# The first layer's output projection as seven half-size products

## The chip, the core and the metric

The kernel runs on one core of a Trainium2 chip. TensorE (PE) multiplies, and its weight loads (PEld) run beside; VectorE (DVE), ScalarE (ACT) and GpSimd (POOL) do everything else on 128-partition tiles, and SyncE (SP) issues the transfers. The metric is the device time of one execution in microseconds, the median of several runs.

## What is computed

Two layers of a diffusion backbone over 512 latent tokens and 256 context tokens of width 1024. The first layer (differential attention) ends, for all 768 tokens, in

```python
o = rms_norm(o, subln_g) * (1.0 - lam_init)
return (o * jax.nn.silu(gate)) @ w_out          # 768 x 1024 times 1024 x 1024
...
x = x + gate * rms_norm(y, post_g[i])           # the same for the context, with cgate
```

and the second layer starts with `h = rms_norm(x, pre_g[i]) * (1.0 + scale) + shift` and its projection to queries, keys, values and gates. The change concerns the product with `w_out` of the first layer.

## The kernel before

**Precision.** Every fp32 operand of a matmul is kept as two parts, a high one (a cast on ACT) and a low one (the difference, a subtraction on DVE or POOL). `mm3` (L142 to L145) multiplies high by high, high by low and low by high into one PSUM tile, so each product of a 128x128 block costs three matmuls.

**Weights.** `WStream` hands out weight tiles in the order in which they were added: `wsplit` loads 512 KB into one of two `raw` buffers (L211, on SP's queue), casts the high part on ACT (L213) and makes the low part with `pieces` (L205 to L207), for `w_out` on DVE. Three slots hold the finished pairs; a fourth comes with the pool `bp`, which is opened when the attention of the first layer has been written out.

**The projection.** The gated attention output is held transposed in eight tiles `gT[0..7]` (128 of the 1024 branch columns by 768 tokens), with high and low parts in `ghi` and `glo` (L1027). `OUTC` cuts the 1024 output columns into three blocks: 0 to 256, 256 to 512 and 512 to 1024. For each block and each of six token tiles of 128 (four latent, two context), 8 column groups `kt` of the contraction times three matmuls fill one PSUM tile. The first block is begun early: `out_early` runs seven of the eight `kt` of all six token tiles among the last head's attention, as filler on PE. The rest follows when `gT[7]` is there.

**After each block.** DVE multiplies the PSUM tile by the layer's gate into `u0` (L1219) or `u1` (L1234), ACT takes the sum of squares (`sumsq`, L1204). In the last block `resid_a` and `resid_b` follow each token tile: POOL forms the reciprocal root (L396, L397), DVE adds the scaled tile to the residual row (L1244), which was loaded from x or the context into `x1`, `gate1` and `gacc` at L1171 and L1174, ACT and POOL normalize that row again for the second layer (L1204, L1250). Two token tiles later `h1_tr` transposes it on PE (L1261), scales and shifts it on DVE and ACT (L1266 to L1269) and splits it (L1271, L1272) into `h1hi` and `h1lo`, the operands of the second layer's projections. That next stage runs in the order of the list `KV`: keys and values of token tile t (`k`, `v`), the late transposes (`t`), finishing steps (`c`) and steps of the second layer's gate (`g`).

**What sets the order.** Within the attention a list scheduler (`flow`) with due times writes out the steps; from the projection on the order is written by hand. A tile framework then places each engine's instructions by a time line of its own, so that the order on an engine can differ from that of the text. On the chip each engine runs its own list strictly in that order and waits on semaphores.

## Time and profile before

| | |
|---|---|
| runs, median (3 runs) | 824.65 us (824.65 to 824.75) |
| span of the profiled execution | 822.0 us |
| median less span | 2.65 us |
| PE busy | 792.7 us (96%) |
| DVE busy | 482.3 us (59%) |
| ACT busy | 457.1 us (56%) |
| POOL busy | 440.4 us (54%) |

The span is that of one execution taken by the hardware profiler, and the runs are timed apart from it; what is left lies outside the first and the last instruction. Busy shares are averages over stages with different limits, so a stage has to be looked at by itself: the projection begins at 459.15 us and the next stage's first projection at 538.07. In rows of the time line the first two numbers are the start and the length in us, then come engine, line of the kernel, operation, output and inputs, shapes and count; in brackets stands the idle time before and what ended it. In rows of groups the numbers behind the bar are busy us and mean ns of one, then the idle time before them. A row of a window has, for each engine, its busy us and its number of instructions, then the granted clock, the share of the DMA engines' time and the GB/s.

### The profile page before, as it was taken

The numbers are of one execution on the slowest core, as the hardware profiler recorded it, in microseconds if no ns is written. First come the engines' busy times: TensorE is split into PE (matmuls) and PEld (weight loads), VectorE is DVE, ScalarE is ACT, GpSimd is POOL, SyncE is SP. The second block draws the span as 40 slices with busy tenths as digits, with TensorE's granted clock in tenths as the row PEclk, the third lists the DMA queues.
The fourth block names the chain that finished last, engine by engine and source line by source line (L and its number), as shares of the span: only waits on it lengthen the run. The fifth ranks groups of instructions, "written<-read, shape, count | busy, mean of one in ns | idle before, by whom it ended". The sixth has DMA issues, their size and how long they took to land. (4 is left out here: it accounts for less than half of the span.)

```text
span 822.0 us, 14412 instructions
## 1 busy us (share of the span) xinstructions
PE 792.7 (96%) x5482; PEld 703.0 (86%) x5482; DVE 482.3 (59%) x896; ACT 457.1 (56%) x1001; POOL 440.4 (54%) x538
## 2 busy tenths in 40 slices
PE   7999999999999999999999999999999999999997
PEld 5678897788887898787988898889999899898986
DVE  3425566754768524675458952579546566755534
ACT  6534357664575544765556852674446576666631
POOL 4544766856367744665822311587788656733101
PEclk9999999999999999999999999999999999999999
DMA  9934211122053321323330045033421210301102
GB/s 300 347 131 142 77 39 52 52 77 90 28 154 98 122 101 65 116 78 118 113 104 26 27 151 182 1 110 103 154 79 52 78 52 1 103 26 52 50 28 103
DMA packets 41540, 77.77 MB, mean 95 GB/s; under 512 B 3584, under 2 KB 18688, under 8 KB 41472
## 3 DMA queue, kind: packets, MB, share of 16 engines
q1 hardware_dynamic: 38048, 71.71, 26.4%
q10 hardware_dynamic: 3424, 5.15, 1.8%
q8 instruction: 43, 0.70, 0.3%
q14 instruction: 25, 0.20, 0.1%
HBM read 70.56 MB, written 2.10 MB: 88 GB/s over the span
## 5 line engine op out<-in xcount | busy, mean ns | idle before, releaser
L207 POOL TENSOR_TENSOR wlo<-raw,whi 128x256 fp32r<-128x256 f32 x200 | 152.0, 792 | 72.8 <-ACT whi L213 63.1
L143 PE MATMUL bk<-whi,h 128*128 128x256 f32 (+1 forms) x592 | 176.9, 302 | 1.1 <-ACT p L1459 0.8
L144 PE MATMUL bk<-wlo,h 128*128 128x256 f32 (+1 forms) x592 | 176.2, 299 | 0.2 <-DVE wlo L207 0.2
L145 PE MATMUL bk<-whi,h 128*128 128x256 f32 (+1 forms) x592 | 175.4, 299 | 0.2 <-DVE h L1272 0.2
L143 PE MATMUL bk<-h,whi 128*128 128x512 f32 (+2 forms) x416 | 147.4, 354 | 2.7 <-ACT sq L979 1.5
L144 PE MATMUL bk<-h,whi 128*128 128x512 f32 (+2 forms) x416 | 144.8, 348 | 0.0
L145 PE MATMUL bk<-h,wlo 128*128 128x512 f32 (+2 forms) x416 | 144.8, 348 | 0.0
L143 PEld LDWEIGHTS bk<-whi,h 128*128 128x128 f32 x592 | 112.6, 191 | 8.2 <-issue 2.8
L145 PEld LDWEIGHTS bk<-whi,h 128*128 128x128 f32 x592 | 112.0, 190 | 4.7 <-issue 0.8
L144 PEld LDWEIGHTS bk<-wlo,h 128*128 128x128 f32 x592 | 112.3, 190 | 3.9 <-DVE wlo L207 0.4
L221 POOL TENSOR_SCALAR p<-p,sm 128x768 f32<-128x768 f32 (+1 forms) x80 | 67.1, 842 | 76.5 <-DVE sm L1460 28.7
L143 PEld LDWEIGHTS bk<-h,whi 128*128 128x128 f32 x416 | 78.2, 188 | 15.1 <-issue 4.0
L213 ACT CAST whi<-raw 128x1024 fp32r<-128x1024 f32 x64 | 67.1, 1048 | 36.1 <-PE bk L144 17.7
L145 PEld LDWEIGHTS bk<-h,wlo 128*128 128x128 f32 x416 | 78.3, 188 | 8.8 <-issue 1.6
L144 PEld LDWEIGHTS bk<-h,whi 128*128 128x128 f32 x416 | 78.4, 188 | 7.2 <-issue 0.8
L888 ACT ACTIVATE p<-sc,sm 128x768 f32<-128x768 f32 (+1 forms) x68 | 59.7, 881 | 37.9 <-DVE sm L885 37.9
L885 DVE TENSOR_REDUCE sm<-sc 128x1 f32<-128x768 f32 (+1 forms) x68 | 60.3, 917 | 17.4 <-PE sc L880 17.3
L181 POOL TENSOR_TENSOR sz<-sz,za 128x384 f32<-128x384 f32 (+1 forms) x24 | 28.1, 1172 | 42.8 <-ACT za L180 42.7
L896 DVE SCALAR_TENSOR_TENSOR p<-p,sm,p 128x768 f32<-128x768 f32 (+1 forms) x34 | 40.1, 1179 | 16.5 <-POOL p L221 14.9
L1480 DVE TENSOR_TENSOR al<-bk,ah 128x512 fp32r<-128x512 f32 x48 | 32.6, 687 | 26.1 <-ACT ah L1479 25.9
L950 ACT CAST ah<-bk 128x512 fp32r<-128x512 f32 x56 | 31.7, 590 | 27.9 <-PE bk L945 24.4
L880 PE MATMUL sc<-qk,qk 64*128 64x384 f32 (+1 forms) x396 | 45.8, 354 | 1.1 <-ACT p L888 1.0
(247 smaller groups left out, 1693.0 us busy)
## 6 DMA issues: line engine op xcount, KB each, us to landing
raw<-in_a_w SPq DMA_DIRECT2D x30, 512.0 KB, 3.6
araw<-in_ada_w SPq DMA_DIRECT2D x12, 1024.0 KB, 5.6
raw<-in_b_w SPq DMA_DIRECT2D x20, 512.0 KB, 3.5
ag<-in_ada_w SPq DMA_DIRECT2D x32, 256.0 KB, 6.9
raw<-in_w_out SPq DMA_DIRECT2D x16, 512.0 KB, 3.5
sw<-qr ACTq DMA_DIRECT2D x32, 128.0 KB, 2.5
gw<-in_ada_w SPq DMA_DIRECT2D x8, 512.0 KB, 3.8
xt<-in_x SPq DMA_DIRECT2D x4, 512.0 KB, 5.3
```

Source lines behind the costliest of these rows:

```text
L143: nc.tensor.matmul(o, ahi, bhi, start=start, stop=False)
L144: nc.tensor.matmul(o, ahi, blo, start=False, stop=False)
L145: nc.tensor.matmul(o, alo, bhi, start=False, stop=stop)
L207: eng.tensor_tensor(dst[:, i:i + n], a[:, i:i + n], b[:, i:i + n], op)
L213: nc.scalar.copy(hi, r)
L221: (nc.vector if eng == "v" else nc.gpsimd).tensor_scalar(dst, src, s_, 1.0, ALU.mult, ALU.mult)
L880: prev = nc.tensor.matmul(sc[m][:, j if nk == T else m, :w], a[r, tok], b[r, c], start=i == 0, stop=i == 2)
L885: nc.vector.tensor_reduce(mx, scv, AX.XY if nk == T else AX.X, ALU.max, negate=True)
L888: nc.scalar.activation(pv_, scv, AF.Exp, bias=mx, accum_out=l[:, m:m + 1])
L896: nc.vector.scalar_tensor_tensor(ps_[0], pt, r, ps_[0], ALU.mult, ALU.add)
L950: nc.scalar.copy(ah, tr)
L1480: nc.vector.tensor_tensor(al, tr, f32(ah), ALU.subtract)
```

## The change

The product is done by a scheme of Strassen's kind. Tokens, contraction and output columns are each cut in two halves (384 tokens, 512, 512), and seven products of 384 x 512 x 512 take the place of eight. Their order is `PRODS = (1, 5, 2, 6, 7, 4, 3)`; each has three token tiles, four `kt` and three matmuls of 512 columns (`prod_mm`). P1 and P2 use quarters of both operands as they are.

- Weights: fourteen half-quarters instead of eight pieces. `wprod` loads a quarter into `raw` (P1, P2, P5, P3) or takes it from six rows `xr`, into which `wq_load` put three quarters; P5, P6, P7 and P3 use sums or differences of quarters, P5's on POOL and the others on DVE (`EPR`). All low parts are made on DVE. The residual rows of x and the context are loaded into the same six rows after P6.
- Left operands: P6, P7 and P4 use differences of the halves of `gT`. `t_split` makes each with a subtraction on DVE, a cast on ACT and a subtraction on DVE, twelve times on 128x384. For P5 `gate_mul` subtracts on POOL in pieces, for heads 0 to 3.
- Results: P1's and P5's PSUM tiles are copied out on ACT (`s1`, `s5`), and P6 goes on accumulating in P1's banks; P6's sums are copied to `u2`. Nine additions of 128x512 on DVE join products (`s1`, `s5`, `u2`). The gate multiply of six of the twelve half rows is done on POOL (`part`).
- `out_early` runs P1 and P5, which need `gT[0..3]` alone.
- The tiles `h1hi`, `h1lo` are each cut in two halves, `h1_tr` lags by `HL = 3` token tiles, and the list `KV` is another.

```diff
-KV = (('k', 0), ('k', 1), ('k', 2), ('k', 3), ('t', 4), ('v', 0), ('v', 1), ('t', 5), ('k', 4), ('c', 0), ...
+KV = (('k', 0), ('t', 3), ('v', 0), ('k', 1), ('t', 4), ('v', 1), ('k', 2), ('t', 5), ('v', 2), ('k', 3), ('c',, ...
+EPR = {1: ('', 'v'), 5: ('p', 'v'), 2: ('', 'v'), 6: ('v', 'v'), 7: ('v', 'v'), 4: ('', 'v'), 3: ('v', 'v')}
+ETS = {2: 'v', 3: 'v', 4: 'v'}
+HL = 3
...
+    def wprod(half, prod, pool, slot, key):
+        def load(kq, nq):
+            r = wp.tile([P, 1024], F32, tag="raw", name=nm("raw"), bufs=2)
+            wq_load(r, kq, nq, half)
+            return r
+
+        es, el = EPR[prod]
+        if prod in (1, 2):
+            r = load(prod - 1, 0)
+        elif prod == 5:
+            r, t = load(0, 1), load(1, 1)
+            pieces(VP[es], r, r, t, ALU.add)
+        elif prod == 6:
+            r = s2w[half] = bp.tile([P, D], F32, tag="xn", name=nm("s2"), bufs=2)
+            pieces(VP[es], r, wq4[0, 1, half], wq4[1, 1, half], ALU.add)
+            pieces(VP[es], r, r, wq4[0, 0, half], ALU.subtract)
+        elif prod == 7:
+            r = wq4[0, 0, half]
+            pieces(VP[es], r, r, wq4[0, 1, half], ALU.subtract)
+        elif prod == 4:
+            r = wq4[1, 1, half]
+        else:
+            r = load(1, 0)
+            pieces(VP[es], r, r, s2w[half], ALU.subtract)
+        hi, lo = w_pair(pool, slot, key)
+        nc.scalar.copy(hi, r)
+        pieces(VP[el], lo, r, f32(hi), ALU.subtract)
+        return hi, lo
+
+    s2w, wq4 = {}, {}
+
+    def wq_load(r, kq, nq, half):
+        k0 = (kq * 4 + half * 2) * P
+        src = w_out[0, k0:k0 + 2 * P, nq * 512:nq * 512 + 512].rearrange("(k p) n -> p k n", p=P)
+        nc.sync.dma_start(r.rearrange("p (k n) -> p k n", k=2), src)
...
-    OUTC = ((0, 256), (256, 256), (512, 512))
+    PRODS = (1, 5, 2, 6, 7, 4, 3)
...
-    add_wout(0)
+    for key in prod_keys(*PRODS):
+        ws.add(key, key[3], key[2])
...
+    def prod_mm(o, w, kt, hi, lo, j, start=False, stop=False, more=False):
+        sl = slice(j * P, (j + 1) * P)
+        wh, wl = w[kt // 2]
+        c = slice((kt % 2) * 512, (kt % 2) * 512 + 512)
+        mm3(o, hi[:, sl], lo[:, sl], wh[:, c], wl[:, c], start, stop, more)
+        yield 3 * 512 / 2400.0
...
+                if h < 4:
+                    pieces(nc.gpsimd, gT[h][:, 384:], gT[h][:, 384:], gT[h][:, :384], ALU.subtract)
...
-            n = OUTC[0][1]
             while len(fillq) > 1 or not {(KT - 2, "o"), KT - 2, "s7"} <= done:
                 yield None
             split_g(range(KT - 1))
-            w_ = get_wout(0, *OUTC[0])
-            w_o.append(w_)
             for ms in ((0, 1), (2, 3), (4, 5)):
                 while ms[0] == 2 and KT - 1 not in sdone:
                     yield None
                 if ms[0] < NQ:
                     sc = sc2()
-                    o_pre.extend(sc[:, j, :n] for j in range(2))
+                    o_pre.extend(sc[:, j, :] for j in range(2))
                 else:
-                    o_pre.extend(pj(n) for _ in range(2))
-                for kt in range(KT - 1):
-                    for m in ms:
-                        yield from out_proj(o_pre[m], ghi, glo, w_, m, n, kt, kt + 1)
+                    o_pre.extend(pj(512) for _ in range(2))
+                for m in ms:
+                    p = m // 3
+                    if p not in w_p:
+                        while not ws.has(*prod_keys(PRODS[p])):
+                            yield None
+                        w_p[p] = get_prod(PRODS[p])
+                    for kt in range(4):
+                        yield from prod_mm(o_pre[m], w_p[p], kt, ghi[kt][:, p * 384:], glo[kt][:, p * 384:], m % 3, kt == 0, kt == 3)
+                    if m == 2:
+                        ws.release(*prod_keys(PRODS[0]))
...
+    def xrow():
+        return h1p.tile([P, D], F32, tag="xr", name=nm("xr"), bufs=6)
...
+    tt = {p: h1half(T) for p in (2, 3, 4)}
...
+    for half in range(2):
+        for kq, nq in ((0, 1), (1, 1), (0, 0)):
+            wq4[kq, nq, half] = xrow()
+            wq_load(wq4[kq, nq, half], kq, nq, half)
+    ws.extend(bp, WX[0], [*prod_keys(*PRODS[2:]), 8, 9, 10, 11])
...
-    for qi, (c, n) in enumerate(OUTC[:2]):
-        w = get_wout(0, c, n) if qi else w_o
-        if qi == 0:
-            for m in order:
-                run(out_proj(o_pre[m], ghi, glo, w, m, n, KT - 1, KT))
-        for m in order:
...
-            nc.vector.tensor_tensor(u0[m][:, c:c + n], o, gate0[v][:, c:c + n], ALU.mult)
...
+    ws.release(*prod_keys(PRODS[1]))
+    lo3, hi3 = slice(0, 384), slice(384, T)
+    tops = {p: [(t[:, i, lo3], t[:, i, hi3]) for i in range(4)] for p, t in tt.items()}
+    tsrc = {2: lambda i: gT[i + 4][:, hi3], 3: lambda i: gT[i][:, lo3], 4: lambda i: gT[i + 4][:, lo3]}
+    spare = h1half(T, F32).rearrange("p a b -> p (a b)")
+    s1 = [spare[:, j * 512:j * 512 + 512] for j in range(3)]
+    s5 = [spare[:, (3 + j) * 512:(4 + j) * 512] for j in range(3)]
+    u2 = [bp.tile([P, 1024], F32, tag="gw", name=nm("u2"), bufs=2) for _ in range(2)]
+    u2 = [u2[j // 2][:, (j % 2) * 512:(j % 2) * 512 + 512] for j in range(3)]
+    b1, b5 = o_pre[:3], o_pre[3:]
+
+    def t_split(p, i):
+        hi, lo = tops[p][i]
+        a, b = {2: (tsrc[2], lambda i: gT[i][:, hi3]), 3: (tsrc[2], tsrc[3]), 4: (tsrc[4], tsrc[2])}[p]
+        VP[ETS[p]].tensor_tensor(tsrc[p](i), a(i), b(i), ALU.subtract)
+        nc.scalar.copy(hi, tsrc[p](i))
+        VP[ETS[p]].tensor_tensor(lo, tsrc[p](i), f32(hi), ALU.subtract)
+
+    for j in range(3):
+        nc.scalar.copy(s1[j], b1[j])
+    for i in range(3):
+        t_split(2, i)
+    for j in range(3):
+        nc.scalar.copy(s5[j], b5[j])
+
+    def part(m, k, v, src, eng):
+        if m not in ss:
+            ss[m] = small(3)
+        sumsq(ss[m][:, 0:1], src, 512)
+        nc.gpsimd.tensor_scalar(ss[m][:, 0:1], ss[m][:, 0:1], EPS, None, ALU.add)
+        u = u0[m, k] = hp.tile([P, 512], F32, tag="gT", name=nm("u0"), bufs=8)
+        eng.tensor_tensor(u, src, gate0[v][:, k * 512:k * 512 + 512], ALU.mult)
+
+    def var(m):
+        return 0 if m < NQ else 1
+
+    def product(o, w, ops, j, kts=range(4), start=False, more=True):
+        for kt in kts:
+            run(prod_mm(o, w, kt, *ops[kt], j, start and kt == 0, kt == 3, more))
+
+    b21 = [(ghi[4 + i], glo[4 + i]) for i in range(4)]
+    b22 = [(ghi[4 + i][:, hi3], glo[4 + i][:, hi3]) for i in range(4)]
+    w = get_prod(2)
+    o2 = [pj(512), pj(512)]
+    for j in range(2):
+        product(o2[j], w, b21, j, range(3), True, False)
+    for i in range(3):
+        t_split(3, i)
+    for j in range(3):
+        if j < 2:
+            product(o2[j], w, b21, j, (3,), more=False)
+        else:
+            o2.append(pj(512))
+            product(o2[j], w, b21, j, range(4), True, False)
+        nc.vector.tensor_tensor(s1[j], o2[j], s1[j], ALU.add)
+        close(o2[j])
+        part(j, 0, 0, s1[j], nc.gpsimd)
+    ws.release(*prod_keys(2))
+    t_split(2, 3)
+    t_split(3, 3)
+    for i in range(4):
+        t_split(4, i)
+    w = get_prod(6)
+    for j in range(3):
+        product(b1[j], w, tops[2], j, range(3))
+    for j in range(3):
+        product(b1[j], w, tops[2], j, (3,))
+        nc.scalar.copy(u2[j], b1[j])
+    ws.release(*prod_keys(6))
+    rows_ = [xrow() for _ in order]
+    x1, gate1, gacc = rows_[:NQ], *rows_[NQ:]
+    for m, t in enumerate(rows_):
+        nc.sync.dma_start(t, x[m * P:(m + 1) * P, :] if m < NQ else xc[(m - NQ) * P:(m - NQ + 1) * P, :])
+    w = get_prod(7)
+    for j in range(3):
+        product(b1[j], w, tops[3], j)
+        nc.vector.tensor_tensor(s5[j], b1[j], s5[j], ALU.add)
+        part(3 + j, 1, var(3 + j), s5[j], nc.gpsimd)
+    ws.release(*prod_keys(7))
+    h1hi, h1lo = htile1(T), htile1(T)
...
     def resid_a(m, o):
-        v = 0 if m < NQ else 1
         u1 = hp.tile([P, 512], F32, tag="gT", name=nm("u1"), bufs=8)
-        sumsq(ss[m][:, 2:3], o, n)
-        nc.vector.tensor_tensor(u1, o, gate0[v][:, c:], ALU.mult)
-        close(o)
-        xn[m] = [u1, rstd_sum(ss[m][:, 2:3], ss[m][:, 0:1])]
+        k = 1 if m < 3 else 0
+        if m >= 3:
+            nc.vector.tensor_tensor(u2[m - 3], o, u2[m - 3], ALU.add)
+            if m > 3:
+                close(o)
+            o = u2[m - 3]
+        sumsq(ss[m][:, 2:3], o, 512)
+        nc.vector.tensor_tensor(u1, o, gate0[var(m)][:, k * 512:k * 512 + 512], ALU.mult)
+        u0[m, k] = u1
+        xn[m] = rstd_sum(ss[m][:, 2:3], ss[m][:, 0:1])
...
     for i, m in enumerate(order):
-        o = pj(n)
-        run(out_proj(o, ghi, glo, w, m, n, 0, 4))
-        if i >= 2:
-            h1_tr(order[i - 2], 0)
-        run(out_proj(o, ghi, glo, w, m, n, 4, 8))
+        p, o, ops = (4, b1[i], tops[4]) if m < 3 else (3, b5[i - 3], b22)
+        if i % 3 == 0:
+            w = get_prod(p)
+        product(o, w, ops, i % 3, range(2))
+        if i >= HL:
+            h1_tr(order[i - HL], 0)
+        product(o, w, ops, i % 3, range(2, 4))
         resid_a(m, o)
-        if i >= 2:
-            h1_tr(order[i - 2], 1)
+        if i >= HL:
+            h1_tr(order[i - HL], 1)
         resid_b(m)
-    ws.release(*wout_keys(0, c, n))
+        if i % 3 == 2:
+            ws.release(*prod_keys(p))
```

More of the change, by code (lines that the diff above doesn't have):

```diff
@@ L193, in w_off @@
         elif key[0] == "o":
-            narrow = dict(OUTC if key[1] == 0 else OUTC1)[key[2]] == 256
+            narrow = key[1] == 1 and dict(OUTC1)[key[2]] == 256
         else:
@@ L244, in fill @@
                 self.items.pop(0)
-                self.ready[key] = wsplit(src, eng, *slot, key)
+                self.ready[key] = (wprod if isinstance(src, int) else wsplit)(src, eng, *slot, key)
         def has(self, *keys):
@@ L266, in tile_backbone, with add_wout1, prod_keys, get_prod @@
     ws = WStream()
-    OUTC = ((0, 256), (256, 256), (512, 512))
+    PRODS = (1, 5, 2, 6, 7, 4, 3)
     OUTC1 = ((0, 256), (512, 512), (256, 256))
-    def add_wout(layer):
-        for c, n in (OUTC, OUTC1)[layer]:
+    def add_wout1():
+        for c, n in OUTC1:
             per = 1024 // n
             for k in range(KT // per):
-                src = w_out[layer, k * per * P:(k + 1) * per * P, c:c + n].rearrange("(k p) n -> p k n", p=P)
-                ws.add(("o", layer, c, k), src, nc.vector)
+                src = w_out[1, k * per * P:(k + 1) * per * P, c:c + n].rearrange("(k p) n -> p k n", p=P)
+                ws.add(("o", 1, c, k), src, nc.vector)
+    def prod_keys(*prods):
+        return [("o", 0, p, half) for p in prods for half in range(2)]
+    def get_prod(p):
+        return [ws.get(k) for k in prod_keys(p)]
     def wout_keys(layer, c, n):
@@ L1145, in tile_backbone @@
         drain()
-        w_o = w_o[0]
     pool_c.close()
@@ L1151, in htile1, with h1half @@
     def htile1(n):
-        return h1p.tile([P, KT, n], F32R, tag="h1", name=nm("h1"), bufs=2)
+        return [h1half(n) for _ in range(2)]
+    def h1half(n, dt=F32R):
+        return h1p.tile([P, 4, n], dt, tag="h1", name=nm("h1"), bufs=4)
     def proj_tok(o, w, t):
@@ L1238, in resid_b @@
     def resid_b(m):
-        u1, r = xn[m][:2]
+        r = xn[m]
         xd = x1[m] if m < NQ else (gate1, gacc)[m - NQ]
         sq = small(2)
-        for j, u in enumerate((u0[m], u1)):
+        for j in range(2):
+            u = u0[m, j]
             sl = slice(j * 512, j * 512 + 512)
@@ L1538, in tail1 @@
             g1hi, g1lo = htile1(512), htile1(512)
-            ghi.extend(g1hi[:, kt, :] for kt in range(KT))
-            glo.extend(g1lo[:, kt, :] for kt in range(KT))
+            ghi.extend(g1hi[kt // 4][:, kt % 4, :] for kt in range(KT))
+            glo.extend(g1lo[kt // 4][:, kt % 4, :] for kt in range(KT))
             split_g1(range(KT - 1))
```

46 lines of the change are left out of this document (11 added, 35 removed).

## Prediction

> **What bounds the kernel now.** I read the page's head, its busy shares and its chain first, then the windows over the stage that is changed.
>
> ```profile
> span 822.0 us, 14412 instructions
> PE 792.7 (96%) x5482; PEld 703.0 (86%) x5482; DVE 482.3 (59%) x896; ACT 457.1 (56%) x1001; POOL 440.4 (54%) x538
> PE 30%; ACT 1%; DVE 1%; issue 0%; POOLq 0%; DVEq 0%; POOL 0%; ACTq 0%
> ```
>
> ```profile
> core 0: us, PE busy (x) PEld busy (x) DVE busy (x) ACT busy (x) POOL busy (x), PEclk, DMA share, GB/s
> 459.15:502.55 43.40, 41.26 (x335) 39.66 (x335) 25.76 (x49) 23.56 (x60) 7.64 (x16) 1.00 0.39 146
> 502.55:540.00 37.45, 37.45 (x183) 30.97 (x182) 20.51 (x34) 20.34 (x53) 16.73 (x33) 1.00 0.14 43
> 540.00:580.00 40.00, 37.38 (x296) 36.11 (x295) 34.35 (x72) 20.55 (x63) 31.99 (x41) 0.96 0.42 127
> 460.00:470.00 10.00, 8.96 (x70) 7.86 (x67) 10.00 (x20) 8.54 (x22) 2.29 (x3) 1.00 0.15 54
> 550.00:552.00 2.00, 2.00 (x12) 2.00 (x11) 1.73 (x6) 0.00 (x0) 2.00 (x3) 0.50 0.66 246
> 552.00:554.00 2.00, 2.00 (x13) 2.00 (x13) 1.42 (x6) 1.97 (x8) 1.84 (x3) 0.64 0.01 2
> ```
>
> TensorE is busy 96% of the span: over the whole kernel every matmul taken out is worth its time, if the others keep up. The first two windows are the projection (first w_out matmul to the next layer's first key/value projection, with the last head's attention among its first 30 us); the third is the stage behind it. PE has 78.7 us of work in the first two, DVE 46.3, so DVE is idle 34.6 us there. But that room is not everywhere: from 460 to 470 DVE is busy the whole 10.00 us, and in the third window 34.35 of 40. The change puts its new work on DVE, so DVE's place in each stretch decides.
>
> **PE's saving.** The two column widths, at their first and last rows of a back-to-back stretch:
>
> ```profile
> 499.83 0.28 PE L144 MATMUL bk<-wlo,h 128*128 128x256 f32 x1
> 502.43 0.28 PE L145 MATMUL bk<-whi,h 128*128 128x256 f32 x1
> 502.55 0.39 PE L143 MATMUL bk<-whi,h 128*128 128x512 f32 x1
> 505.81 0.39 PE L145 MATMUL bk<-whi,h 128*128 128x512 f32 x1
> ```
>
> There are 22 starts from 499.83 to 502.43 (0.1182 us each) and 14 from 502.55 to 505.81 (0.2329 each). Before: 6 token tiles x 8 x 3 matmuls twice at 256 columns (288) and once at 512 (144): 288 x 0.1182 + 144 x 0.2329 = 67.6 us. After: 7 products x 3 token tiles x 4 x 3 = 252 at 512: 58.7 us. PE loses **8.9 us**.
>
> **What DVE gets.** Back-to-back rows give its price by width:
>
> ```profile
> 490.07 1.41 DVE L1219 TENSOR_TENSOR u<-bk,gate 128x256 f32<-128x256 f32 x4
> 459.54 2.69 DVE L1027 TENSOR_TENSOR h<-gT,h 128x768 fp32r<-128x768 f32 x3
> L207 DVE TENSOR_TENSOR wlo<-raw,whi 128x1024 fp32r<-128x1024 f32 x9 | 11.0, 1220 | 5.4 <-ACT whi L213 5.3
> ```
>
> 0.35 us for 256 and 0.90 for 768 make 0.08 + 1.07 ns an element: 0.49 at 384, 0.63 at 512, 1.17 at 1024 (the row's 1.22 is that with the fill of a lone one). Added: 24 of 384 in t_split (11.8), 6 more low parts of weights (14 halves for 8; 7.0), 8 weight sums of 1024 (9.4), 9 PSUM additions of 512 (5.7); gone: six halves' gate multiplies, now on POOL (-4.2). Net +29.7: DVE 76.0 against PE 69.8 in this stretch. DVE becomes the longer one even at no idle moment, and over all three windows it needs 80.6 + 29.7 = 110.3 of 112. I therefore walk the queues: each engine runs its instructions in the order the built program gives them, so I take that order and these prices.
>
> **S1, attention of the last heads.** P5's weights are a sum of two quarters on POOL (raw<-raw,raw, four pieces a half). It stands ahead of a sigmoid multiply, a softmax scale and a square sum:
>
> ```profile
> 441.16 1.23 DVE L207 TENSOR_TENSOR wlo<-raw,whi 128x1024 fp32r<-128x1024 f32 x1 [1.36 <-ACT whi L213]
> 442.42 22.13 SPq L211 DMA_DIRECT2D raw<-in_w_out  x2
> raw<-in_w_out SPq DMA_DIRECT2D x5, 512.0 KB, 3.8
> x<-in_x SPq DMA_DIRECT2D x4, 512.0 KB, 5.0
> L207 POOL TENSOR_TENSOR wlo<-raw,whi 128x256 fp32r<-128x256 f32 x16 | 13.2, 862 | 0.1
> 445.86 1.02 POOL L181 TENSOR_TENSOR sz<-sz,za 128x384 f32<-128x384 f32 x1 [2.08 <-ACT za L180]
> 446.86 0.90 POOL L221 TENSOR_SCALAR p<-p,sm 128x768 f32<-128x768 f32 x1
> 447.73 1.00 POOL L380 TENSOR_TENSOR sqs<-sq,sqs 128x384 fp32r<-128x384 f32 x1
> 451.57 0.45 PE L143 MATMUL bk<-h,whi 128*128 128x384 f32 x1 [1.47 <-ACT sq L979]
> ```
>
> Both raw buffers hold P1's halves, so the second operand's load is issued when the low part at 441.16 ends (442.42, as the next load of before) and lands 3.8 later (446.2); 4 x 0.86 end at 449.6; the three rows then end at 452.5, not 448.7. PE's column sum of the square (its 1.47 wait at 451.57 hangs on it) has about 1 us to spare: **+2.7**.
>
> **S2, the last head.** Seven t_split instructions of 384 come in DVE's order ahead of the last head's softmax multiply, in the stretch where DVE has no idle moment:
>
> ```profile
> 469.02 0.47 DVE L896 SCALAR_TENSOR_TENSOR p<-p,sm,p 128x256 f32<-128x256 f32 x1
> 465.07 0.38 PE L145 MATMUL sc<-whi,h 128*128 128x256 f32 x1 [0.43 <-DVE h L1027]
> 469.16 0.51 PE L150 MATMUL bk<-al,vhi 128*128 128x256 f32 x2 [0.49 <-DVE al L951]
> 470.59 0.39 PE L143 MATMUL sc<-whi,h 128*128 128x256 f32 x1 [0.72 <-ACT p L888]
> ```
>
> 7 x 0.49 = 3.4 us. P5's second pair sum on POOL (load issued behind another low part, 4 x 0.86 of work) lies ahead of the other half's scale and costs about as much on its own path, beside it. PE, already 2.7 late, no longer waits 0.43 + 0.49 + 0.72 = 1.64: **+1.8**, S1 and S2 together +4.5. Bounds 2 (POOL's sum slips into its idle stretch) to 7 (both add up).
>
> **S3.** P2's second half takes a slot in the pool that opens only behind the attention's tail, as the weights did on which PE waits at 487.93 in before. The low part on which it waits ended there at 487.9; with 4.5 this is 492.4, and DVE has two more low parts and a subtraction of 384 ahead of it (2 x 1.17 + 0.49 = 2.8), so 495.2. Two old waits go (0.22 and 0.29):
>
> ```profile
> 487.93 0.39 PE L144 MATMUL bk<-wlo,h 128*128 128x256 f32 x1 [0.22 <-DVE wlo L207]
> 491.11 0.38 PE L143 MATMUL bk<-whi,h 128*128 128x256 f32 x1 [0.29 <-ACT jk L1204]
> ```
>
> 2.8 - 0.5: **+2.3** (0 to 4; 0 if DVE does them in a pause of the tail).
>
> **S4, the main term.** Behind that low part DVE's order has 14 t_split of 384 (6.9), 3 PSUM additions of 512 (1.9) and 11 of 1024 (12.9: weight sums of P6, P7 and, early, of P3, and low parts) before the low part of P6's second half is done: 21.7 us, to 516.9. The low part of P6's first half is the sixth of the 1024s and comes at 511.0. PE has until then only 22 matmuls of P2 and the first 14 of P6: 36 x 0.2329 = 8.4 us. It runs 10, waits about 2.2 for a PSUM bank that one of the additions frees, runs 14, waits 8.0 for P6's first half, runs 12 and waits 3.1 for the second: 21.7 - 8.4 = **+13.3**. None of the 21.7 us waits for PE except the additions; what moves it is only whether DVE did part of it earlier, and the order puts it behind. Below: 8 (the sums' loads have landed long before, ACT's casts lie beside). Above: 17 (the casts between, at 1.05 each, exposed).
>
> **S5, token 0's way to the next layer.** The transposes of normalized row 0 come when this chain is done:
>
> ```profile
> 511.16 0.60 ACT L1204 ACTIVATE jk<-bk 128x512 bf16<-128x512 f32 x1 [6.62 <-PE bk L145]
> 516.16 1.13 POOL L1250 TENSOR_SCALAR xn<-x,sm 128x1024 f32<-128x1024 f32 x1
> ```
>
> 6.1 us in all. After, DVE's residual stands behind P3's first PSUM addition, from where 18 matmuls (4.2 us) remain before the transposes, against some 5.3 of the chain; P3's weights wait 0.4 for the slots of P7: **+1.5** (0 to 4). The x and xc loads move behind P6 on SP's queue; at 5.0 us a load token 0's row is there before P7's 36 matmuls (8.4) are done, and no load that PE needs soon stands behind them: 0, or 3 if the six share the transfer rate to the last.
>
> **S6, the stage behind.** DVE's left-overs meet a window that is 86% full on it already: I count 53 us of DVE work against 39.5 of PE until the backlog ends. The order of key and value projections is laid for it, and PE's waits of before there (2.5 us) go: **+1** (-2 to 7).
>
> **S7, the clock.** The two windows at 550 show granted clocks of 0.50 and 0.64: 1.0 + 0.72 = 1.7 us lost, just after this wait:
>
> ```profile
> 547.53 0.63 PE L1261 MATMUL sc<-ident,gate 128*128 128x128 f32 x4 [1.31 <-POOL wlo L207]
> ```
>
> One such dip behind the 8 us stall: **+1.7** (0 to 5, if each of three stalls has one). The Trainium skill (TensorE: Matmul & The Clock Gate, Part 1) puts the half clock behind an idle window of about 3.4 us; by it the 8 us stall alone counts, +1.7 again, yet the trace has its dip behind a far shorter wait, so the upper end stays.
>
> Hidden: the 8 further loads of 512 KB (DMA share 0.39 and 0.14); POOL's 16 pieces for heads 0 to 3 (POOL idle 46% of the span; 0 to 2 us); the PSUM copies on ACT (43.9 busy of 80.9).
>
> **Sum.** 4.5 + 2.3 + 13.3 + 1.5 + 1.0 + 1.7 = 24.3, less 8.9: +15.4. Runs of before have a median of 824.65, 2.65 over the profiled span; that rest stays. **840.0 us** (824.65 + 15.4).
>
> **Rivals.**
> *DVE keeps up* (faster). The sums need only loads that have landed early, and DVE's idle 34.6 us are there. If 13 or more of S4's 21.7 us are done before PE ends P2, its stalls are gone and with them the dip; with S1 left, 824.65 - 8.9 + 2.7 = 818.5. Against it: the fixed order, and 98% of DVE needed. Chance 0.12.
> *Only the DVE stretch stalls.* The attention's late steps and the tail are absorbed: -8.9 + 13.3 + 1.7 = +6.1, 830.8. For it: POOL has nothing to do right after 448.73; against: DVE full from 460. Chance 0.12.
> *POOL slows DVE.* Six gate multiplies of 512 run on POOL beside the sums. One pair of rows shows a DVE instruction held for POOL's whole multiply, the other none:
>
> ```profile
> 454.56 1.86 POOL L839 TENSOR_TENSOR gT<-gT,sz 128x768 f32<-128x768 f32 x1 [0.89 <-DVE sm L891]
> 454.59 1.85 DVE L895 TENSOR_TENSOR sm<-sm,nlam 128x1 f32<-128x1 f32 x1
> 467.00 1.48 POOL L181 TENSOR_TENSOR sz<-sz,za 128x384 f32<-128x384 f32 x1 [4.12 <-ACT za L180]
> 466.67 0.94 DVE L1027 TENSOR_TENSOR h<-gT,h 128x768 fp32r<-128x768 f32 x1
> ```
>
> Six times about 1.35 held: +8, 848. The second pair is the nearer in kind, so 0 is in the sum. The Trainium skill (GPSIMD Engine Reference, 1. Specifications) says that POOL shares its SBUF interfaces with DVE and that instructions with two SBUF inputs contend; by it this rival holds. Chance 0.08.
> That the matmuls are not saved is excluded: the built program has 252.
>
> **How the numbers follow.** Forecast 0.66 (its own range 833 to 848 by S3, S4 and S6), rivals 0.12, 0.12, 0.08, and 0.02 for landing within 0.2% (1.65 us, about what a measurement of this kernel can tell). Slower 0.86, faster 0.12. The range leaves out the faster rival and the far top: 826 to 851.
>
> **What would show it.** Right: no DVE idle from about 493 to 517, PE waits on DVE additions and on the low parts of P6 summing to 13, a sum on POOL ahead of the scale near 450. Wrong: those DVE instructions found before 490, or P6 starting within 2 us of P2's end; then the time falls below before's.

## The result: 863.6 us, 4.6% slower, and the profile after

The changed kernel takes 863.59 us (862.77 to 864.17, 4 runs) against 824.70 in the same session: a ratio of 1.0461, 95% interval 1.0446 to 1.0477. The prediction had the sign and less than half of the size: 840.0, in a range of 826 to 851. The profiled execution took 864.17 us with a span of 862.4, so 1.8 us lie outside it.

The head of the page after, its busy shares and its chain:

```profile
span 862.4 us, 14142 instructions
PE 799.8 (93%) x5302; PEld 698.7 (81%) x5302; DVE 516.4 (60%) x931; ACT 472.8 (55%) x1016; POOL 470.0 (55%) x554
PE 27%; DVE 3%; ACT 2%; POOL 2%; issue 1%; DMA 1%; POOLq 0%; DVEq 0%; ACTq 0%
```

PE is busy 7 us longer with 180 matmuls fewer: part of them ran at half clock. The following windows of the kernel after begin at the same transposes of the second last head (431.38 us before, 433.84 after) and end at the first gate projection of the next stage (593.48 before, 634.25 after). They are cut in P2, behind the wait for P6's second low part, and at P3's first low part. Then come the windows of before, cut behind the last wait in its projection and at the projection's end.

```profile
core 0: us, PE busy (x) PEld busy (x) DVE busy (x) ACT busy (x) POOL busy (x), PEclk, DMA share, GB/s
433.84:497.08 63.24, 54.62 (x308) 46.90 (x309) 48.10 (x80) 36.00 (x74) 23.38 (x22) 0.92 0.16 51
497.08:526.55 29.47, 15.64 (x46) 10.97 (x47) 26.74 (x34) 15.64 (x31) 11.17 (x5) 0.77 0.50 168
526.55:543.74 17.19, 16.67 (x71) 12.73 (x69) 5.62 (x7) 6.45 (x9) 3.37 (x4) 1.00 0.34 110
543.74:634.25 90.51, 74.04 (x504) 68.50 (x505) 62.02 (x124) 47.64 (x134) 62.17 (x92) 0.91 0.36 107
```

```profile
431.38:493.00 61.62, 58.01 (x438) 54.46 (x439) 47.49 (x83) 40.85 (x92) 14.92 (x18) 1.00 0.18 67
493.00:538.07 45.07, 45.07 (x247) 38.60 (x246) 20.81 (x35) 20.89 (x55) 16.00 (x36) 1.00 0.26 90
538.07:593.48 55.41, 52.79 (x425) 51.52 (x424) 41.42 (x88) 28.41 (x85) 43.38 (x59) 0.97 0.42 132
```

The length less PE's busy time is PE's waiting. Busy time lost to a lower clock I added up over windows of 2 us (busy times one minus the granted clock). The rest is work at full clock:

| | waiting | lost to the clock | work |
|---|---|---|---|
| before, 162.1 us | 6.2 | 1.7 | 154.2 |
| after, to 497.08 | 8.6 | 3.4 | 51.2 |
| after, P2 to P6 (to 526.55) | 13.8 | 3.9 | 11.8 |
| after, P6 and P7 (to 543.74) | 0.5 | 0 | 16.7 |
| after, P4, P3 and the next stage | 16.5 | 6.2 | 67.8 |
| after, 200.4 us | 39.4 | 13.5 | 147.5 |

So the stretch is 38.3 us longer: 33.2 more waiting, 11.8 more at a lower clock, 6.7 less work. The whole span is 40.4 us longer: 2.5 more lie ahead of the stretch and 0.4 less behind it. In the profiles of the other versions of the changed kernel the same transposes begin between 432.0 and 434.0, so part of the 2.5 is scatter between executions; the subtractions on POOL for heads 0 to 3, which also lie there, were not told apart from it. These are the waits of PE in the kernel after on which the argument rests, as rows of the time line (the idle time and what ended it in brackets):

```profile
454.21 0.44 PE L428 MATMUL bk<-sqs,ones_r 128*128 128x384 f32 x1 [1.84 <-POOL sqs L426]
455.38 0.45 PE L146 MATMUL bk<-h,whi 128*128 128x384 f32 x1 [0.73 <-ACT sq L1034]
474.72 0.50 PE L153 MATMUL bk<-al,vhi 128*128 128x256 f32 x2 [0.92 <-DVE al L1006]
476.95 0.80 PE L427 MATMUL bk<-sqs,ones_r 128*128 128x512 f32 x1 [1.73 <-ACT sqs L425]
480.28 0.48 PE L1000 MATMUL bk<-ident,p 128*128 128x128 f32 x1 [2.54 <-DVE p L951]
497.08 0.50 PE L146 MATMUL bk<-whi,h 128*128 128x512 f32 x1 [0.56 <-ACT sq L1049]
499.84 0.50 PE L146 MATMUL bk<-whi,h 128*128 128x512 f32 x1 [1.10 <-ACT whi L245]
501.10 0.50 PE L147 MATMUL bk<-wlo,h 128*128 128x512 f32 x1 [0.54 <-DVE wlo L210]
507.03 0.51 PE L146 MATMUL bk<-whi,h 128*128 128x512 f32 x1 [3.35 <-DVE h L1321]
520.30 0.80 PE L147 MATMUL sc<-wlo,h 128*128 128x512 f32 x1 [8.20 <-DVE wlo L210]
525.98 0.50 PE L147 MATMUL sc<-wlo,h 128*128 128x512 f32 x1 [0.64 <-DVE wlo L210]
557.08 0.66 PE L1386 MATMUL sc<-ident,xn 128*128 128x128 f32 x4 [2.40 <-POOL xn L1375]
562.36 0.79 PE L146 MATMUL sc<-whi,h 128*128 128x512 f32 x1 [4.62 <-DVE u L1358]
572.80 0.63 PE L1386 MATMUL sc<-ident,xn 128*128 128x128 f32 x4 [2.19 <-ACT hf L1394]
589.32 0.44 PE L146 MATMUL bk<-whi,h 128*128 128x256 f32 x1 [3.57 <-DVE vl L1499]
610.82 0.58 PE L146 MATMUL bk<-whi,h 128*128 128x256 f32 x1 [2.90 <-DVE vl L1499]
```

The waits from 507 to 526 are those of the prediction's S4 (3.35 + 8.20 + 0.64 = 12.2, forecast 13.3). Those from 557 on are the tail, which the prediction had at 2.5 us. DVE's list behind the S4 waits and the loads it needs, in rows of DVE's and SP's time lines:

```profile
498.48 3.03 SPq L254 DMA_DIRECT2D xr<-in_w_out  x6
499.82 1.23 DVE L210 TENSOR_TENSOR wlo<-raw,whi 128x1024 fp32r<-128x1024 f32 x1
504.68 1.23 DVE L210 TENSOR_TENSOR s<-xr,xr 128x1024 f32<-128x1024 f32 x1 [1.76 <-DMA xr<-in_w_out]
508.62 5.08 DVE L1283 TENSOR_TENSOR h<-gT,h 128x384 fp32r<-128x384 f32 x6
519.04 1.21 DVE L210 TENSOR_TENSOR wlo<-s,whi 128x1024 fp32r<-128x1024 f32 x1
524.71 1.21 DVE L210 TENSOR_TENSOR wlo<-s,whi 128x1024 fp32r<-128x1024 f32 x1
```

From the end of P2's low part (501.05) to the end of P6's second (525.92) DVE needs 24.9 us, its only pause being 1.76. The prediction said 21.7. That pause, for six rows that are loaded only at 498.48 and not long before as I wrote, and six splits at 0.85 us instead of 0.49 (2.1 us) make up the difference of 3.2 and 0.7 more. PE was later too, so the waits came out 1.1 shorter.

### The profile page after: what moved, and what is told of

Same layout as the page of the kernel before. It is cut to its first block, busy times and chain, and to the rows that moved or that the text cites. A ratio compares the mean times of both kernels' runs of the same rounds, so it can differ in the third digit from the quotient of the medians.

```text
span 862.4 us, 14142 instructions
## 1 busy us (share of the span) xinstructions
PE 799.8 (93%) x5302; PEld 698.7 (81%) x5302; DVE 516.4 (60%) x931; ACT 472.8 (55%) x1016; POOL 470.0 (55%) x554
## 5 line engine op out<-in xcount | busy, mean ns | idle before, releaser
L146 PE MATMUL bk<-whi,h 128*128 128x256 f32 (+1 forms) x508 | 154.0, 307 | 12.4 <-DVE vl L1499 6.5
L147 PE MATMUL bk<-wlo,h 128*128 128x256 f32 (+1 forms) x508 | 152.9, 302 | 1.1 <-DVE wlo L210 1.1
L148 PE MATMUL bk<-whi,h 128*128 128x256 f32 (+1 forms) x508 | 151.4, 301 | 0.6 <-DVE h L1397 0.6
L146 PEld LDWEIGHTS bk<-whi,h 128*128 128x128 f32 x508 | 98.5, 195 | 21.0 <-DVE vl L1499 7.2
L260 POOL TENSOR_SCALAR p<-p,sm 128x768 f32<-128x768 f32 (+1 forms) x80 | 69.6, 873 | 72.4 <-DVE sm L1588 28.0
L147 PEld LDWEIGHTS bk<-wlo,h 128*128 128x128 f32 x508 | 98.6, 194 | 4.6 <-DVE wlo L210 1.9
L148 PEld LDWEIGHTS bk<-whi,h 128*128 128x128 f32 x508 | 97.7, 193 | 4.6 <-issue 0.8
L216 ACT CAST whi<-raw 128x1024 fp32r<-128x1024 f32 x56 | 58.5, 1046 | 33.6 <-PE bk L147 15.9
```

The lines of the kernel that those rows point to most:

```text
L146: nc.tensor.matmul(o, ahi, bhi, start=start, stop=False, skip_group_check=more)
L147: nc.tensor.matmul(o, ahi, blo, start=False, stop=False, skip_group_check=more)
L148: nc.tensor.matmul(o, alo, bhi, start=False, stop=stop, skip_group_check=more)
L216: nc.scalar.copy(hi, r)
L260: (nc.vector if eng == "v" else nc.gpsimd).tensor_scalar(dst, src, s_, 1.0, ALU.mult, ALU.mult)
```

## The experiments

Theory A is the prediction's: DVE's list in order sets the middle, and a slower tail comes from each token tile's chain of steps, with less PE work beside it. Rivals: B, late loads; C, POOL and DVE hold each other up; D, a backlog of the other engines sets the tail whatever PE does there; and the clock as a cost of its own. A difference below is (ratio of the run less 1.0461) x 825 us, since sessions differ by up to 1 us; each ratio is to the kernel before in its own session.

**The middle.** Without the eight weight sums:

```diff
-            pieces(VP[es], r, wq4[0, 1, half], wq4[1, 1, half], ALU.add)
-            pieces(VP[es], r, r, wq4[0, 0, half], ALU.subtract)
+            r = s2w[half] = wq4[0, 1, half]        # and P7, P3 likewise
```

> Left out: the eight weight sums of 128x1024 on DVE (P6, P7 and P3 multiply by plain quarters of w_out; P5's sum on POOL stays, loads and low parts stay). The changed kernel lost 8.20 us in one wait for P6's low part. Theory A (DVE's own list between P2 and P6 sets that wait): six sums of 1.21 us go ahead of P6's last low part, the wait of 8.2 shrinks to about 1 and the half-clock stretch behind it goes: 7 to 11 us less, about 854. Theory B (what DVE lacks there is the late loads of the quarters, issued at 498.5): the low parts still wait for them, 3 us less at most, 860 or more. Theory C (POOL and DVE hold each other up): no more than 3 us less.

858.81 us, ratio 1.0381 (1.0334 to 1.0428): 6.6 less by the ratios, but 4.8 by the medians, since one of the four runs, at 852.49, lies 6 us below the others. That is short of A and more than the 3 us that B and C allow, though the interval reaches down to 2.7. The 8.20 shrank to 4.25, since the splits of 384 still stand ahead of the low part. Without `t_split`:

```diff
-        VP[ETS[p]].tensor_tensor(tsrc[p](i), a(i), b(i), ALU.subtract)
-        nc.scalar.copy(hi, tsrc[p](i))
-        VP[ETS[p]].tensor_tensor(lo, tsrc[p](i), f32(hi), ALU.subtract)
+        pass                                       # tops: plain halves of ghi, glo
```

> Left out: t_split (24 DVE subtractions of 128x384 and 12 ACT casts); P6, P7 and P4 multiply plain halves that exist already. Theory A: seven of the 24 stand ahead of the last head's softmax multiply and fourteen ahead of P6's low parts: about 3 us of the last head's waits and 7 of P6's go, with one or two half-clock stretches: 10 to 15 us less, about 851. Theory B (late loads): only the last head's 3 us, about 860. Theory C: under 3 us less.

857.26, ratio 1.0381 (1.0366 to 1.0397): 6.6 less, short of the 10 to 15 expected of A. With both left out:

> Both left out (the eight weight sums on DVE and all of t_split). Theory A with the tail as a stage of its own: the last head's and P6's waits go (about 3 and 12 us) and three half-clock stretches (5 to 6 us), the waits from P4 on (9.3 and 7.2 us in the profile, with three half-clock stretches) stay: 840 to 846, still 15 to 21 over the kernel before. Rival D (DVE's backlog from the middle is what makes the tail late): the tail's waits go too, and the time falls to 825 or below.

845.28, ratio 1.0241 (1.0223 to 1.0260): 18.2 less, as A had it, and more than the two added (13.2): each alone leaves the other's work ahead of P6's low parts. No wait at P6 is left, although the rows are loaded as late as ever, so B is out as more than the 1.76 us. The tail is nearly unmoved: from P3's first low part to the first gate projection PE waits 15.0 us, in the changed kernel 16.5. The longest of these waits (others of 1.83 and 1.23 are not shown):

```profile
521.68 0.50 PE L147 MATMUL bk<-wlo,h 128*128 128x512 f32 x1 [0.53 <-DVE wlo L210]
535.00 0.71 PE L1381 MATMUL sc<-ident,xn 128*128 128x128 f32 x4 [2.39 <-POOL xn L1370]
540.28 0.80 PE L146 MATMUL sc<-whi,h 128*128 128x512 f32 x1 [4.56 <-DVE u L1353]
568.56 0.38 PE L146 MATMUL bk<-whi,h 128*128 128x256 f32 x1 [3.69 <-DVE vl L1494]
```

The 2.39, 4.56 and 3.69 are the 2.40, 4.62 and 3.57 of the changed kernel. The tail is a stage of its own, and DVE's work in the middle is not its cause.

**The clock.** Added before P6:

```diff
+    od = pj(384)
+    for _ in range(FILL):                       # FILL = 40
+        nc.tensor.matmul(od, ghi[4][:, :P], ghi[5][:, hi3], start=True, stop=True)
+    close(od)
```

> Added: 40 matmuls of 384 columns (7.0 us at full clock) into a spare PSUM bank between P2 and P6; nothing is left out. If PE's 8.20 us ahead of P6's low part are idle and the half clock behind it (windows 520 to 524) costs 2 us or more, the added 7 us cost nothing and the time falls by 1.5 to 3 us, about 861. If the half clock costs nothing on the path: same, 863.6. If the stall is not PE's to give (PE is late itself): up to 7 us more, 870.

863.93, ratio 1.0462 (1.0444 to 1.0480): no change. The 7 us of matmuls went into the idle time, and the clock stayed up; the gain did not come. PE's rows and windows of this kernel:

```profile
509.58 7.12 PE L1328 MATMUL bk<-h,h 128*128 128x384 f32 x40
518.41 0.50 PE L148 MATMUL sc<-wlo,h 128*128 128x512 f32 x1 [1.24 <-DVE wlo L211]
524.09 0.50 PE L148 MATMUL sc<-wlo,h 128*128 128x512 f32 x1 [2.65 <-DVE wlo L211]
509.00:518.00 9.00, 8.17 (x45) 7.64 (x43) 9.00 (x12) 1.74 (x3) 2.93 (x4) 0.98 0.17 60
518.00:524.00 6.00, 3.03 (x12) 2.17 (x12) 6.00 (x7) 2.13 (x3) 6.00 (x1) 1.00 0.35 105
```

The clock is 1.00 after the wait, and the next wait, for P6's second low part, is 2.65 us instead of 0.64: what PE gained in speed it waited. DVE (6.00 of 6.00) sets both. The same for the last long wait of the next stage:

```diff
+                od = sc2()[:, 0, :]
+                for _ in range(m):              # m = 12
+                    nc.tensor.matmul(od, h1lo[1][:, 3, 5 * P:], h1hi[1][:, :, 5 * P:], start=True, stop=True)
```

> Added: 12 matmuls of 512 columns (2.8 us at full clock) in the next stage's last long wait (2.90 us at 610.8), behind which the granted clock is 0.5 to 0.6 for 6 us, and no further wait follows for 40 us. If that half clock lies on the path, the filled wait keeps the clock up and the time falls by 1.5 to 3 us, about 861. If the half clock comes whatever PE does there, the same 863.6. If the wait is shorter than the filling, up to 2 us more.

865.65, ratio 1.0489 (1.0464 to 1.0515): 2.3 more, which the intervals do not tell from no change. The first window is of the changed kernel, the second, at the same work, and the rows are of this one:

```profile
610.00:616.00 6.00, 5.18 (x24) 5.19 (x25) 4.44 (x9) 1.04 (x1) 3.48 (x5) 0.50 0.50 158
```

```profile
611.00:616.00 5.00, 4.49 (x37) 4.27 (x37) 4.83 (x9) 2.47 (x5) 4.19 (x5) 1.00 0.54 163
611.73 0.39 PE L146 MATMUL bk<-whi,h 128*128 128x256 f32 x1 [0.51 <-DVE vl L1503]
619.92 0.39 PE L146 MATMUL bk<-whi,h 128*128 128x256 f32 x1 [1.80 <-DVE kl L1464]
```

The clock goes from 0.50 to 1.00, the wait of 2.90 to 0.51, and 8 us later PE waits 1.80 for DVE again. Ahead of P6, then, the time "lost to the clock" is waiting in another form and not a cost beside it. The second place is less clean: this run's profile has another dip, at 573 to 577 (granted clock 0.71 and 0.50 in windows of 2 us), which the changed kernel does not have. Whether any of the other five dips is on the path was not tried.

**The tail.** First the order of the next stage alone, on the kernel before:

```diff
-KV = (('k', 0), ('k', 1), ...
+KV = (('k', 0), ('t', 3), ('v', 0), ...            # as in the changed kernel
-        if i >= 2:
+        if i >= 3:                                  # and h1_tr(order[i - 3], ...)
```

> The kernel before with only the new order of the next stage (list KV) and transposes three token tiles later (HL = 3). Theory A (the tail is late because P4 and P3 give each token tile half the cover of before): here every token tile keeps its 24 matmuls of 512, so the order alone is worth little: 823 to 829. Rival (the new order of the next stage is itself the cost of the tail): 835 or more, up to 843.

829.94 against 825.84, ratio 1.0048 (1.0033 to 1.0063): 4 us slower, 1 beyond A's range and far from the rival's: on the kernel before the order itself costs a little. The reverse, on the changed kernel (old list, `HL = 2`):

> The changed kernel with the order of the next stage (list KV) and the lag of the transposes (HL = 2) of the kernel before. On the kernel before, the new order alone cost 4.1 us. If it costs the same here (it serves nothing in the tail), 859 to 860. If it is what the halved cover needs (row 0 normalized 2.40 us late already with the longer lag), the first transposes come one token tile earlier and wait longer: 866 to 870.

873.18, ratio 1.0578 (1.0554 to 1.0602): 9.7 more, beyond the 866 to 870 of the second case. So the new order and the longer lag, which this run takes back together, serve the changed kernel: without them its tail is worse. Which of the two does it is not shown. Doubling PE's work in P4 and P3:

```diff
-        product(o, w, ops, i % 3, range(2))
+        for _ in range(2):
+            product(o, w, ops, i % 3, range(2))     # and the other two kt likewise
```

> Each of the 72 matmuls of P4 and P3 is done twice: 16.8 us more work for PE, 5.6 us per token tile as in the kernel before. Theory A (each token tile's chain needs some 5 us and has only 2.8 us of PE beside it): 9 to 13 of the 16.8 us fall into waits that are there anyway, 867 to 871. Rival (the tail's waits hang on DVE's backlog or on the order of the next stage, behind P3): all of it is added, 878 to 881.

881.37, ratio 1.0672 (1.0655 to 1.0690): 17.4 more for 16.8 us of work, as the rival had it. By the time nothing was hidden, so **my theory of halved cover fell**. Over the stretch of the table PE waits 37.8 us here and 39.4 in the changed kernel; in the tail the waits stand behind the longer products (1.65 and 3.50, both for the gate multiply L1358, then 1.10, 0.99, 3.56, 1.35 and 2.97). The run does not show that more cover is of no use to a chain that starts in time: ACT's first square of a token of P4 starts here only at 555.29, after 8.85 us of waiting for PE, so the longer products also start the chains later. The banks:

```diff
-    b1, b5 = o_pre[:3], o_pre[3:]
+    b1, b5 = [o_pre[2], o_pre[0], o_pre[1]], o_pre[3:]   # out_early fills them in that order
```

> Only the PSUM banks of P1, P6, P7 and P4 are dealt out differently, so that the tile of two banks which P3's first token shares holds token 0 and not token 2. The changed kernel waits 4.62 us at P3's first token for token 2's gate multiply, which DVE does third. If that shared tile is the reason, the wait goes, and what comes next is the wait for row 0's normalization (2.40 us there): 3 to 6 us less, 858 to 860. If the chain of each token tile through ACT, POOL and DVE sets the tail whatever stands in the banks, the same time within 1.5 us, and the wait stands later.

859.57, ratio 1.0405 (1.0388 to 1.0423): 4.6 less. The first of these rows of this kernel shows row 0's transposes waiting 0.16, not 2.40, and the 4.62 is gone; the wait at the third transposes is 6.58, not 2.19:

```profile
559.17 0.66 PE L1386 MATMUL sc<-ident,xn 128*128 128x128 f32 x4 [0.16 <-POOL xn L1375]
568.08 1.12 PE L1386 MATMUL sc<-ident,xn 128*128 128x128 f32 x4 [6.58 <-ACT hf L1394]
```

So the shared tile of two banks was a real cause, and by the rows not of the 4.62 alone. P4's first two tokens share a tile of two banks as well. In the changed kernel ACT's first square of a token of P4, with which row 0's chain begins, starts at 549.68, when a product of PE ends, although the first token's own product had ended by 542.8. With the banks swapped it starts 3 us earlier, behind other work of ACT (the first row is of the changed kernel, the second of this one):

```profile
549.68 0.60 ACT L1265 ACTIVATE jk<-sc 128x512 bf16<-128x512 f32 x1 [4.03 <-PE sc L148]
546.60 0.58 ACT L1265 ACTIVATE jk<-sc 128x512 bf16<-128x512 f32 x1
```

That the other token in the tile held this square back is read from the rows and was not tested by itself. Most of the waiting came back at later steps: in all PE waits 14.8 us in the tail of this run's profile, in the changed kernel's 16.5. The time lost to the clock fell more, from 6.2 to 2.4, so some dips of the tail may have been on the path. Leaving out the second norm:

```diff
-            sumsq(sq[:, j:j + 1], xd[:, sl], 512)
...
-        r = rstd_sum(sq[:, 1:2], sq[:, 0:1])
```

> Left out: the normalization of the new residual row (two ACT squares, the POOL additions and root; the row is multiplied by the first root instead). That takes some 2.8 us of ACT and POOL out of the chain of each of six token tiles. Theory A (chain of each token tile): the waits of the tail (2.40, 4.62, 2.19, 3.57, 2.90) shrink together by 6 to 10 us, 852 to 858. Rival (DVE's backlog alone sets the tail): DVE's work is the same, within 2 us of 863.6.

858.51, ratio 1.0400 (1.0376 to 1.0424): 5.0 less, short of the 6 to 10 that A expected and more than the 2 that its rival allows. Leaving out the gate's accumulation (`('g', 0)` out of `KV`):

> Left out: the 16 DVE steps of 128x512 that add up the second layer's gate in the next stage (0.74 us each, 12 us of DVE) and six of their eight loads. Theory D (DVE's backlog sets the waits of the next stage: 3.57 and 2.90 us on low parts of values, which stand behind such steps): 3 to 6 us less, 858 to 860. Theory A (the rows of the last three token tiles come late, one after the other, through ACT, POOL and DVE): the 3.57 us stay, since these steps come behind it in DVE's list, and at most the 2.90 go: 861 to 863.

858.94, ratio 1.0405 (1.0386 to 1.0424): 4.6 less, as D had it; the 2.90 is gone and, as A had it, the 3.57 stays (3.56). The gate multiplies on DVE:

```diff
-        part(j, 0, 0, s1[j], nc.gpsimd)
+        part(j, 0, 0, s1[j], nc.vector)             # and P7's three
```

> The six gate multiplies of 128x512 go from POOL to DVE (3.8 us more for DVE, six times 1.7 us less for POOL). Theory C (POOL and DVE hold each other up: 2.33 us for two residual steps that take 1.41 elsewhere, 2.09 us for a row that takes 1.13): 3 us less or more than that, 860 or below. Theory A (DVE's list sets the middle): the three of P2 stand before or among P6's low parts and add up to 2 us, the three of P7 nothing: 863 to 866.

864.47, ratio 1.0478 (1.0454 to 1.0501): 1.4 more, not told from no change, as A had it. What C names exists, but moving the multiplies is no way to gain. POOL's rows of the changed kernel, then a DVE row of this one:

```profile
519.20 9.01 POOL L1298 TENSOR_TENSOR u<-h,gate 128x512 f32<-128x512 f32 x1 [5.90 <-DVE h L1321]
537.98 1.29 POOL L1298 TENSOR_TENSOR u<-h,gate 128x512 f32<-128x512 f32 x1 [9.50 <-DVE h L1343]
```

```profile
507.59 2.89 DVE L1283 TENSOR_TENSOR h<-gT,h 128x384 fp32r<-128x384 f32 x6
```

Beside DVE's unbroken list a multiply of POOL took 9.01 us, alone 1.29; and the six splits that took DVE 5.08 beside two of them take 2.89 without. Those 2.2 us are about what DVE then pays for the three multiplies of P2 itself.

**Do the parts add up?** The cause of the tail was still open, so four more runs. All parts out (sums, differences, gate, second norm, with the swapped banks):

> Left out at once: the eight weight sums on DVE, t_split, the gate's accumulation and the second norm; with the swapped banks. Singly these gave 4.8, 6.3 (18.3 together), 4.7, 5.1 and 4.0 us. If middle and tail are stages of their own and the parts of the tail add up: 863.6 - 18.3 - 13.8 = 831.5. If the parts of the tail hide each other: 836 to 841. If they were one and the same backlog of DVE: below 828.

833.74, ratio 1.0109 (1.0084 to 1.0135): 29.0 less, where the single differences add up to 18.2 + 4.6 + 4.6 + 5.0 = 32.4. That lies between the first two cases: if the middle gives its 18.2 here too, the tail's three give 10.8 together instead of 14.2. Even so PE waits 12.2 us in this run's tail, against 2.6 in the same stage before. Its two longest waits, and DVE's list ahead of the second:

```profile
544.00 1.11 PE L1377 MATMUL sc<-ident,xn 128*128 128x128 f32 x4 [6.01 <-ACT hf L1385]
550.98 0.58 PE L148 MATMUL bk<-whi,h 128*128 128x256 f32 x1 [5.01 <-DVE h L1388]
544.10 5.69 DVE L1364 SCALAR_TENSOR_TENSOR xr<-u,sm,xr 128x512 f32<-128x512 f32 x6
```

The low part that PE waits for there (L1388) starts at 549.71, right behind these six residual additions. No run moved them. With P5's pair sum out as well:

```diff
-            r, t = load(0, 1), load(1, 1)
-            pieces(VP[es], r, r, t, ALU.add)
+            r = load(0, 1)
```

> As g1, and P5 multiplies by a plain quarter (no pair sum on POOL, one load less for each half). By the prediction's first step the pair sum costs 2.7 us ahead of the column sum, by the trace 1.1 (waits of 1.84 and 0.73 for 1.47): 1 to 3 us below g1. If nothing hangs on it, g1's time.

832.54, ratio 1.0087 (1.0070 to 1.0103): 1.8 less by the ratios, 1.2 by the medians; the intervals overlap. The last three rows ahead of P3:

```diff
+        if i == 3:
+            for e in (3, 4, 5):
+                resid_b(e)                          # root: a constant; P7's half twice
```

> The residual rows of token tiles 3 to 5 are formed ahead of P3 from sums that are there already (a constant in the place of the root, P7's half twice): the same number of DVE, ACT and POOL instructions, but the rows do not wait for P3. If the tail is late because these three rows come one by one after P3's end: 8 to 12 us less, 852 to 856. If DVE's backlog sets the tail whatever the rows wait for: within 3 us of 863.6.

863.05, ratio 1.0460 (1.0437 to 1.0483): no change. These rows wait for P3, but with the other waits of the changed kernel in place that costs nothing. The two parts that cost no work, together:

> Nothing left out: the swapped banks (-4.0 alone), and the eight steps of the gate's accumulation stand at the end of the list of the next stage. If DVE's backlog in that stage is only moved behind what PE waits for: 3 us or more below the swapped banks alone, 855 to 857. If it then delays what follows: 859 to 862.

860.28, ratio 1.0426 (1.0409 to 1.0444): no better than the swapped banks alone, as the second case had it. The accumulation can be dropped to a profit but not moved to one.

## Why the prediction was wrong

**PE's saving** (8.9): 6.7 by the table, 252 matmuls being there. A few per cent of the records can be missing, so this is no more exact than that.

**S1 and S2** (4.5 together): without the waits that belong to S3, PE waits 8.1 up to 497.08 against 3.1 before, 5.0 more: close to the sum, but split otherwise, so that it fits is in part luck. P5's pair sum ran in 0.70 a piece, not 0.86. POOL's rows after answer to those before:

```profile
448.54 2.81 POOL L210 TENSOR_TENSOR raw<-raw,raw 128x256 f32<-128x256 f32 x4 [2.32 <-issue]
453.17 0.99 POOL L426 TENSOR_TENSOR sqs<-sq,sqs 128x384 fp32r<-128x384 f32 x1
```

S1 is 1.84 + 0.73 - 1.47 = 1.1 us in place of 2.7, and leaving the sum out gave 1.2 to 1.8, not told from nothing. The last head makes up for it (2.54 on `p`, 1.73, 0.92). Two dips of the clock there (3.4 us) were not forecast.

**S3** (2.3): 0.56 (for the sum of squares at 497.08), 1.10 and 0.54, less 0.5: 1.7. The size is right, the mechanism in part: only the 0.54 is a wait for P2's low part, the other two are for ACT.

**S4** (13.3): 12.2, as waits of 3.35, 8.20 and 0.64 where 2.2, 8.0 and 3.1 were forecast. The right step for the right reason: taking away DVE's sums and splits takes 18.2 us. In the profile of that run the stretch up to P3's first low part is 20.3 us shorter, 14.7 by waiting and 5.4 by the clock, which is S4 with its dips and a part of S2. The rival by which DVE would have spread them could not be, since their rows are loaded at 498.48.

**S5 and S6** (1.5 and 1.0) are **the step that failed**: 2.5 us forecast, and PE waits 16.5 there against 2.6, with 6.2 at a lower clock against 1.7: 18.4 us more. I followed row 0 alone, compared its chain with PE's matmuls, took the rest as covered, and read the new list `KV` as a remedy. S6 had counted 53 us of DVE's work against 39.5 of PE's, 13.5 more, and still put +1, with no reason but that order; PE's waits grew by 13.9. That these two agree is no proof, for DVE is not full there (62.02 of 90.51 us, POOL 62.17), and 12 us of DVE's work taken out gave 4.6. Row 0's transposes did wait 2.40, but its chain began some 7 us after its product and not right behind it. What I missed, with what each was worth alone: a PSUM tile of two banks that P3's first token shares with the token whose gate multiply comes third (4.6), the second norm in each row's chain (5.0), the gate's accumulation between the steps PE waits for (4.6); and that the new order itself costs 4 us on the kernel before. Doubling PE's products hid nothing, and taking away the wait of the last rows for P3 changed nothing. The three together gave 10.8 us of the tail's 18; what the rest hangs on is open.

**S7** (1.7): the profile has 11.8. The row at 550 had said that a dip follows waits of 1.3 us; I kept that for the upper end and took one dip, and there were seven. But the dip ahead of P6, where it was tried, lies in front of the next wait for DVE and costs nothing of its own, so a larger term there would have counted the same time twice. For the dips of the tail this is open.

**The rivals.** "Only the DVE stretch stalls" and "DVE keeps up" failed on the tail and on S4. "POOL slows DVE" named a thing that is there (2.2 us on six splits, not 8 in all). No version tried beats the kernel before: with DVE's sums and splits left out it takes 845.3, and with the gate's accumulation, the second norm and the pair sum out as well and the banks swapped 832.5, which is still slower.

## What to carry to other kernels

A saving on the engine that is 96% busy counts only as far as every other engine's list has room in the very stretch, in order. DVE's 34 idle us were of little use to it: the rows for its sums were loaded only at 498.48, and in the 17.19 us behind P6's last wait, too late for P6, DVE was idle 11.6. When a change also rearranges what comes after (banks, lags, orders of the next stage), that stage must be walked through to its end like the changed one: about half of the loss was there, spread over several steps. And a half-clock stretch behind a wait is not to be added to the waits before it is seen whether another wait follows.

## What the runs showed of the hardware

PE's clock fell to 0.50 behind waits much shorter than the one for which I had reckoned: behind 2.90 us at 610.82 for 6 us, and behind waits of 1.84 and 0.73 in this window of the kernel after:

```profile
456.00:460.00 4.00, 4.00 (x16) 4.00 (x15) 3.97 (x8) 4.00 (x8) 1.93 (x1) 0.57 0.00 0
```

The Trainium skill (TensorE: Matmul & The Clock Gate, Part 1) puts this behind an idle window of about 3.4 us; the measured waits are shorter, so as a bound for a single wait it does not hold here. That PE kept busy keeps the clock agrees with it (1.00 in place of 0.50).

Beside DVE's instructions with two inputs a POOL multiply took 9.01 us that takes 1.29 alone, and six splits of DVE took 0.85 each beside two POOL multiplies and 0.48 without. The Trainium skill (GPSIMD Engine Reference, 1. Specifications) names these as the ones that contend; the trace agrees, and most of the price was POOL's.
